# Token operands of the first MLP projection taken from PSUM in product order, and a new issue order of stores and loads between the two projections

## The chip, the core and the metric

The kernel runs on one core of one Trainium2 chip. The metric is device time in microseconds (us) of one execution; the median of the runs is what is compared. The engines are called by their names: TensorE (PE in the profile, its weight loads PEld), VectorE (DVE), ScalarE (ACT), GpSimd (POOL) and SyncE (SP), whose queue issues every DMA of this kernel.

## What is computed

One layer of a hybrid trunk over 1024 tokens of width 1024, in float32. A token mixer (causal pooling groups and a chunked gated delta net) comes first; nothing of it changes here. The part in question is what follows it:

```python
h = h + mix @ w_out
u = rms_norm(h, norm_mlp)                              # 1024 tokens x 1024
h = h + square(relu(u @ w_up)) @ w_down                # 1024 x 4096, then back
return rms_norm(h, norm_final)
```

## The kernel before, in words

**Products.** Each float32 matrix product is made of three passes on TensorE: an operand is split into a rounded part (`wh`, `th`) and the rest (`wl`, `tl`), both in a 32-bit matmul format, and `mm3` multiplies high by high, high by low and low by high. Each of the two MLP projections is done by a scheme with seven block products in place of eight (as Strassen's and Winograd's): the 2 x 2 blocks are the two halves of the tokens (512 each), of the contracted dimension and of the outputs.

**First projection.** The 4096 hidden units come in 16 pairs `p` of 2 x 128. A product is called (p, i), i = 1 to 7: four blocks of 128 rows, three matmuls each, so 12 matmuls of 128 x 128 by 128 x 512. Its weights are made per product by `up_ready`: sums and differences of the four blocks of the raw tile `wu` (in place), then `split` into `wh` (ScalarE cast, L932) and `wl` (VectorE subtraction, L933). Its tokens, `TH[i]` and `TL[i]`, are made once and serve all pairs. `TH[1], TL[1], TH[2], TL[2]` come from the first half of the tokens (`turn_first`). The other five need the second half: `turn_second` turns the normalised tokens `xn` with 32 matmuls on the identity (L48) into eight PSUM banks, ScalarE copies each bank out, weighed by the norm (L914, tiles `r12` and `r22`), VectorE and GpSimd form the differences (L916 and L918 on VectorE, L919 and L920 on GpSimd), and for each i ScalarE casts to `th` (L926) and VectorE subtracts to `tl` (L927).

**Order.** TensorE's queue is in program order. The other engines' queues were put in order by a scheduler when the program was built, and each runs strictly in that order. The list `order` says: (0,1), (1,1), (0,2), (1,2), then the turn, then 6, 7, 5, 4, 3 for pairs 0 and 1 in turn; from pair 2 on 1, 6, 2, 7, 5, 4, 3. A pair has three accumulating banks; the ends of the products give `p1`, `h11`, `u2`, `u3`, `s1`, `s2`, `s4`, which are stored to a DRAM scratch `hd` by `keep` (L960). Small tiles come from the pool `cp` ("c", 9 buffers).

**Second projection.** For i = 1, 2, 5, 6, 7, 3, 4 and eight steps s each, `down_load` brings the raw weights `w` (512 KB, L1069) and the stored hidden values `x` (512 KB, from `hd`, L1072). Both, like the stores, stand in SyncE's one queue. The first step (1, 0) is split in halves (`wh`, `wl`), the others whole (`sh`, `sl`, `th`, `tl`).

Of the kernel before, what the change touches and what calls it, by code (L numbers as in the profile page):

```python
# [28 lines left out]
def hybrid_trunk(ctx, tc, x, norm_mix, w_in, conv_w, w_pool, pool_scale, a_log, dt_bias,  # L29
# [859 lines left out]
    R[12], R[2] = (u3(f"r{n}", F32) for n in (12, 2))  # L889

# [11 lines left out]

    def turn_second(ys):

        R[22] = [c_tile("r22") for _ in range(4)]

        def block(r, j):
            return R[22][j] if r == 22 else R[r][:, j, :]
# [12 lines left out]
        for i, r in ((6, 2), (7, 12), (5, 11), (4, 21), (3, 22)):  # L921
            TH[i] = (big_tile(f"th{i}", [4, HALF], F32R) if i in (5, 4) else
                     u2p.tile(ub, F32R, name="th3", tag="r21") if i == 3 else u3(f"th{i}", F32R))
            TL[i] = big_tile("tl3", [4, HALF], F32R) if i == 3 else u3(f"tl{i}", F32R)
            for j in range(4):
                A.copy(TH[i][:, j, :], block(r, j))  # L926
                V.tensor_tensor(TL[i][:, j, :], block(r, j), TH[i][:, j, :].bitcast(F32), op=ALU.subtract)  # L927
# [14 lines left out]
    def up_ready(p, i):  # L942

        r = raws[p]
        a11, a12, a21, a22 = r[:, :4, :P], r[:, 4:, :P], r[:, :4, P:], r[:, 4:, P:]
        if i == 1:
            G.tensor_tensor(a21, a21, a22, op=ALU.add)
        if i == 6:
            G.tensor_tensor(a11, a21, a11, op=ALU.subtract)
        src = {1: a11, 2: a12, 3: a12, 4: a22, 5: a21, 6: a11, 7: a11}[i]  # L950
        if i == 7:
            G.tensor_tensor(a11, a22, a11, op=ALU.subtract)
        out = split(src, [P, 4, P], ws, "wh", "wl", 5)
        made2.add((p, i))
        if i in (2, 6) and {(p, 2), (p, 6)} <= made2:
            G.tensor_tensor(a12, a12, a11, op=ALU.subtract)
        return out

    def keep(p, i, t):
        nc.sync.dma_start(out=hd[p // 2][i][:, p % 2, :], in_=t)  # L960
# [5 lines left out]
    def combine(p):  # L966

        m = tmp.pop(p)
        h11, h21, h22, h12 = m["h11"], m["p1"], m["u3"], m["u2"]
        s1, s2, s4 = c_tile("s1"), c_tile("s2"), c_tile("s4")  # L970
        V.tensor_tensor(s1, h12, h22, op=ALU.add)
        keep(p, 5, s1)
        V.tensor_tensor(s2, s1, h11, op=ALU.subtract)
        keep(p, 6, s2)
        V.tensor_tensor(h12, h11, h12, op=ALU.subtract)
        keep(p, 7, h12)
        V.tensor_tensor(s4, h21, s2, op=ALU.subtract)
        keep(p, 3, s4)

    def up_product(p, i, w):  # L980
# [14 lines left out]
        elif i == 6:  # L995
            m["u2"] = ws.tile([P, HALF], F32, name="u2", tag="raw", bufs=3)
            V.tensor_tensor(m["u2"], acc, m["p1"], op=ALU.add)
        elif i == 7:
            m["u3"] = c_tile("u3") if p == 1 else ws.tile([P, HALF], F32, name="u3", tag="raw", bufs=3)
            V.tensor_tensor(m["u3"], acc, m["p1"], op=ALU.add)  # L1000
        elif i == 5:
            V.tensor_tensor(m["u3"], acc, m["u3"], op=ALU.add)
            hidden(m["u3"], m["u3"])
            keep(p, 4, m["u3"])
        elif i == 4:
# [3 lines left out]
        else:  # L1009
            V.tensor_tensor(m["u2"], acc, m["u2"], op=ALU.add)  # L1010
            hidden(m["u2"], m["u2"])
# [7 lines left out]
    first = {}  # L1019
    for n, e in enumerate(order):  # L1020
        if e != "turn" and e[0] not in first:
            first[e[0]] = n
# [22 lines left out]
    close(cpc)  # L1045
# [10 lines left out]
    w2c, w2 = opened(name="wr2", bufs=4, reuse_waits="tile")  # L1056
# [96 lines left out]
    close(w2c)  # L1153
# [34 lines left out]
```

## Time and profile before

| | us |
|---|---|
| median of 3 runs | 1172.87 (1172.27 to 1178.7) |
| the profiled execution | 1173.46 |
| its span in the trace | 1171.7 |
| TensorE busy | 1099.8 (94%) |
| VectorE busy | 786.6 (67%) |
| ScalarE busy | 602.8 (51%) |
| GpSimd busy | 327.1 (28%) |

The first projection runs from 514 us to 851 us of the span, the second from there to the end. A row of the timeline has the start, the duration, the engine, the line, the operation and, in brackets, how long the engine had been idle before it and what ended that. Where a row ends in x4 or the like, four instructions in a row are merged, and the duration is from the start of the first to the end of the last. Busy matmul time overlaps itself (a matmul of 0.39 us starts 0.23 us after the one before), so a product is measured from start to start.

### The profile page before, as it was taken

To read this page: it belongs to the slowest core of one execution; us is meant where nothing else is said; L and a number is where in the kernel's file an instruction comes from. 1 tells how busy PE (TensorE), PEld (TensorE's weight loads), DVE (VectorE), ACT (ScalarE), POOL (GpSimd) and SP (SyncE) were. 2 spreads that over 40 slices of the span, in tenths; PEclk is the share of its full clock that TensorE was granted. 3 is DMA by queue.
4 is the path that set the end of the run, shared out by engine and by line. 5 is a ranking of instruction groups with operands and counts; after the bars stand their busy time and mean duration, and the time that the engine had idled before them with its cause. 6 is when DMAs were issued, how large, how long until landed. Compare 5 with 4: busy or idle time off the path is not lost.

```text
span 1171.7 us, 15587 instructions
## 1 busy us (share of the span) xinstructions
PE 1099.8 (94%) x5606; PEld 893.7 (76%) x5606; DVE 786.6 (67%) x1224; ACT 602.8 (51%) x1117; POOL 327.1 (28%) x288
## 2 busy tenths in 40 slices
PE   6998999988898999995999999999979999999997
PEld 5777777767687788773788888888868888888886
DVE  5698698878879775559646454545455597465584
ACT  6666566566565554635545454545443333334353
POOL 7033365465754431045132323131100000000010
PEclk9999999999999999997999999999989999999999
DMA  5233211111213321121344444444298797256561
GB/s 161 81 101 116 61 52 41 55 55 43 66 41 126 109 72 37 37 72 54 133 155 153 147 150 152 145 153 145 81 361 294 262 394 242 90 195 192 189 215 72
DMA packets 93047, 155.23 MB, mean 132 GB/s; under 512 B 7781, under 2 KB 45738, under 8 KB 92970
## 3 DMA queue, kind: packets, MB, share of 16 engines
q1 hardware_dynamic: 92970, 154.24, 39.1%
q8 instruction: 44, 0.72, 0.2%
q14 instruction: 33, 0.27, 0.1%
HBM read 120.66 MB, written 33.55 MB: 132 GB/s over the span
## 4 chain that ended last, share of the span: by engine, by line
PE 71%; DVE 12%; ACT 3%; issue 2%; POOL 2%; DMA 0%; POOLq 0%; DVEq 0%; ACTq 0%; SPq 0%
PE bank L44 53%; PE acc L44 17%; DVE cy L391 2%; DVE tl L927 1%; DVE nxt L410 1%; DVE xx L592 1%; PE bank L48 1%; DVE nxt L409 0%; DMA x<-hd 0%; DVE r L918 0%; ACT th L172 0%; DVE ul L173 0%; DVE ml L764 0%; DVE m L546 0%; DVE kn L533 0%
## 5 line engine op out<-in xcount | busy, mean ns | idle before, releaser
L44 PE MATMUL bank<-th,wh 128*128 128x512 f32 x448 | 178.3, 398 | 11.7 <-ACT th L926 10.7
L44 PE MATMUL bank<-tl,wh 128*128 128x512 f32 x448 | 178.1, 398 | 3.0 <-DVE tl L927 2.9
L44 PE MATMUL bank<-th,wl 128*128 128x512 f32 x448 | 177.5, 396 | 2.2 <-DVE wl L933 2.2
L932 ACT CAST sh<-x 128x1024 fp32r<-128x1024 f32 x55 | 57.9, 1054 | 160.9 <-PE bank L44 154.2
L44 PE MATMUL bank<-th,sh 128*128 128x512 f32 x344 | 133.8, 389 | 0.0
L44 PE MATMUL bank<-th,sl 128*128 128x512 f32 x344 | 133.8, 389 | 0.0
L44 PE MATMUL bank<-tl,sh 128*128 128x512 f32 x344 | 133.8, 389 | 0.0
L44 PE MATMUL acc<-uh,wh 128*128 128x512 f32 x320 | 130.4, 407 | 1.1 <-DVE ul L173 0.6
L44 PE MATMUL acc<-ul,wh 128*128 128x512 f32 x320 | 129.3, 404 | 0.0
L932 ACT CAST wh<-wu 128x512 fp32r<-128x512 f32 x112 | 69.1, 621 | 116.0 <-PE bank L44 98.2
L44 PE MATMUL acc<-uh,wl 128*128 128x512 f32 x320 | 128.8, 402 | 0.0
L933 DVE TENSOR_TENSOR sl<-x,sh 128x1024 fp32r<-128x1024 f32 x55 | 67.3, 1223 | 88.1 <-ACT sh L932 88.0
L933 DVE TENSOR_TENSOR wl<-wu,wh 128x512 fp32r<-128x512 f32 x112 | 80.4, 722 | 45.0 <-ACT wh L932 45.0
L44 PEld LDWEIGHTS bank<-th,wh 128*128 128x128 f32 x448 | 85.1, 190 | 32.0 <-ACT th L926 11.4
L44 PEld LDWEIGHTS bank<-tl,wh 128*128 128x128 f32 x448 | 85.0, 190 | 24.5 <-DVE tl L927 5.4
L44 PEld LDWEIGHTS bank<-th,wl 128*128 128x128 f32 x448 | 85.1, 190 | 22.3 <-DVE wl L933 3.1
L152 POOL TENSOR_TENSOR stf<-stf,mhalf 128x1 f32<-128x1 f32 x8 | 7.9, 998 | 329.7 <-DVE stf L1125 329.7
L588 POOL TENSOR_TENSOR bl<-m,lev 128x512 f16<-128x512 f16 x48 | 62.0, 1291 | 82.5 <-PE bank L44 70.2
L391 DVE SCALAR_TENSOR_TENSOR cy<-cr,cols,cy 128x512 f32<-128x512 f32 x72 | 74.1, 1034 | 8.2 <-ACT cy L389 7.7
L133 POOL TENSOR_TENSOR wl<-raw,wh 128x512 fp32r<-128x512 f32 x48 | 68.0, 1421 | 36.4 <-ACT wh L132 36.2
L44 PEld LDWEIGHTS bank<-th,sl 128*128 128x128 f32 x344 | 64.6, 188 | 13.5
L44 PEld LDWEIGHTS bank<-th,sh 128*128 128x128 f32 x344 | 64.6, 188 | 13.5
(325 smaller groups left out, 2372.1 us busy)
## 6 DMA issues: line engine op xcount, KB each, us to landing
w<-in_w_down_dram SPq DMA_DIRECT2D x72, 512.0 KB, 6.9
x<-hd SPq DMA_DIRECT2D x56, 512.0 KB, 3.3
raw<-in_w_in_dram SPq DMA_DIRECT2D x80, 256.0 KB, 2.7
wu<-in_w_up_dram SPq DMA_DIRECT2D x16, 1024.0 KB, 5.4
hd<-s SPq DMA_DIRECT2D x48, 256.0 KB, 2.0
hd<-u SPq DMA_DIRECT2D x32, 256.0 KB, 2.1
raw<-in_w_out_dram SPq DMA_DIRECT2D x24, 256.0 KB, 2.8
xin<-in_x_dram SPq DMA_DIRECT2D x8, 512.0 KB, 5.1
```

The source lines that it names most:

```text
L44: T0.matmul(out, lhsT, rhs, start=start, stop=stop, skip_group_check=goes_on)
L48: T0.transpose(out, in_, identity)
L133: eng.tensor_tensor(lo, raw, hi.bitcast(F32), op=ALU.subtract)
L152: last["rsqrt"] = G.tensor_tensor(s, s, mhalf[:, :n], op=ALU.pow)
L391: V.scalar_tensor_tensor(cy, cr[:, e:e + HALF], tap[e], cy, op0=ALU.mult, op1=ALU.add)
L410: V.tensor_tensor(nxt[:, n:], cur[:, n:], cur[:, :W - n], op=ALU.add)
L588: G.tensor_tensor(bl, m1, bc(lev[l]), op=ALU.mult)
L592: V.tensor_tensor(xx, px, bc(ident), op=ALU.add)
L927: V.tensor_tensor(TL[i][:, j, :], block(r, j), TH[i][:, j, :].bitcast(F32), op=ALU.subtract)
L932: A.copy(hi, src)
L933: V.tensor_tensor(lo, src, hi.bitcast(F32), op=ALU.subtract)
```

## The change

In `up_ready` the sums and differences of the weight blocks are moved from GpSimd to VectorE for pairs 0 and 1, and the weight parts of (0,1) and (1,1) come from the "c" pool. `turn_second` stands ahead of (0,2) and (1,2) now. The differences are taken by VectorE straight from PSUM, in one instruction that weighs the bank and subtracts (`weighed`, L908), and operand 3 is split from PSUM (`weigh`, L172 and L173). The operands are made in the order 6 with 3, then 5, 7, 4, by functions that stand between the products; GpSimd has none of it. The order of the products is 6, 5, 3, 7, 4 for pairs 0 and 1 and 1, 6, 2, 5, 7, 3, 4 from pair 2 on, with `v5` in the place of `u3`. Of the last pair only the first store is issued at once, the others are kept for after the first loads of the second projection, and the pool `w2` of that projection is opened at its first use.

```diff
+TH[3], TL[3], TH[6], TL[6] = (u3(nm, F32R) for nm in ("th3", "tl3", "th6", "tl6"))
+def weighed(r, k, x):
+    V.scalar_tensor_tensor(r, turned_banks[k], nmlp[:, k:k + 1], x, op0=ALU.mult, op1=ALU.subtract)
+def parts_of(i, src):
+    for j in range(4):
+        A.copy(TH[i][:, j, :], src[j])
+        V.tensor_tensor(TL[i][:, j, :], src[j], TH[i][:, j, :].bitcast(F32), op=ALU.subtract)
 def turn_second(ys):
     for k in range(KT):
-        pt = acc_bank() if k < 2 else work_bank()
+        pt = turned_banks[k] = acc_bank() if k in (0, 1, 6, 7) else work_bank()
         turn(ys, k, pt)
         j = k % 4
-        A.activation(block(12 if k < 4 else 22, j), pt, AF.Copy, scale=nmlp[:, k:k + 1])
         if k < 4:
-            V.tensor_tensor(R[11][:, j, :], R[12][:, j, :], R[11][:, j, :], op=ALU.subtract)
+            A.activation(R[12][:, j, :], pt, AF.Copy, scale=nmlp[:, k:k + 1])
+            weighed(R[11][:, j, :], k, R[11][:, j, :])
         else:
-            V.tensor_tensor(R[2][:, j, :], R[22][j], R[11][:, j, :], op=ALU.subtract)
-            G.tensor_tensor(R[12][:, j, :], R[22][j], R[12][:, j, :], op=ALU.subtract)
-            G.tensor_tensor(R[21][:, j, :], R[21][:, j, :], R[2][:, j, :], op=ALU.subtract)
-    for i, r in ((6, 2), (7, 12), (5, 11), (4, 21), (3, 22)):
...
+            weighed(R[2][:, j, :], k, R[11][:, j, :])
+    parts_of(6, rows_of(2))
+    for j in range(4):
+        weigh(turned_banks[4 + j], 4 + j, TH[3][:, j, :], TL[3][:, j, :], nmlp)
+def operands_5():
+    TH[5], TL[5] = (big_tile(f"t{m}5", [4, HALF], F32R) for m in "hl")
+    parts_of(5, rows_of(11))
+def operands_7():
+    for j in range(4):
+        weighed(R[12][:, j, :], 4 + j, R[12][:, j, :])
+    R[4] = [c_tile("r4") for _ in range(4)]
+    for j in range(4):
+        V.tensor_tensor(R[4][j], R[21][:, j, :], R[2][:, j, :], op=ALU.subtract)
+    TH[7], TL[7] = u3("th7", F32R), big_tile("tl7", [4, HALF], F32R)
+    parts_of(7, rows_of(12))
+def operands_4():
+    TH[4], TL[4] = u2p.tile(ub, F32R, name="th4", tag="r21"), u3("tl4", F32R)
+    parts_of(4, R[4])
 def up_ready(p, i):
+    eng = V if p < 2 else G
     if i == 1:
-        G.tensor_tensor(a21, a21, a22, op=ALU.add)
+        eng.tensor_tensor(a21, a21, a22, op=ALU.add)
...
+    if i == 1 and p < 2:
+        out = split(src, [P, 4, P], cp, "c", "c", 9)
+    else:
+        out = split(src, [P, 4, P], ws, "wh", "wl", 5)
...
 def keep(p, i, t):
+    if p == NPAIR - 1 and i != 1:
+        late.append((p, i, t))
+    else:
+        store(p, i, t)
...
-order = [(0, 1), (1, 1), (0, 2), (1, 2), "turn"]
-order += [(0, 6), (1, 6), (0, 7), (1, 7), (0, 5), (1, 5), (0, 4), (1, 4), (0, 3), (1, 3)]
+order = [(0, 1), (1, 1), lambda: turn_second(ys), (0, 2), (1, 2), operands_5, (0, 6), (1, 6), operands_7,
+         (0, 5), (1, 5), (0, 3), (1, 3), operands_4, (0, 7), (1, 7), (0, 4), (1, 4)]
 for p in range(2, NPAIR):
-    order += [(p, i) for i in (1, 6, 2, 7, 5, 4, 3)]
+    order += [(p, i) for i in (1, 6, 2, 5, 7, 3, 4)]
...
-w2c, w2 = opened(name="wr2", bufs=4, reuse_waits="tile")
+            if n and "w2" not in pools:
+                close(cpc)
+                pools["w2c"], pools["w2"] = opened(name="wr2", bufs=4, reuse_waits="tile")
...
+        while late:
+            store(*late.pop(0))
```

VectorE's queue around the operand of product 6, before: `tl6` is the low part of that operand, `r11`, `r2` and `r22` are differences and weighed blocks, `tl7` and `tl5` the low parts for products 7 and 5.

```order
L916 TENSOR_TENSOR r11_5485<-r12_5783,r11_5485 128x512 x4
L918 TENSOR_TENSOR r2_5784<-r22_5944,r11_5485 128x512
L918 TENSOR_TENSOR r2_5784<-r22_5945,r11_5485 128x512
L918 TENSOR_TENSOR r2_5784<-r22_5946,r11_5485 128x512
L918 TENSOR_TENSOR r2_5784<-r22_5947,r11_5485 128x512
L927 TENSOR_TENSOR tl6_6013<-r2_5784,th6_6012 128x512 x4
L927 TENSOR_TENSOR tl7_6023<-r12_5783,th7_6022 128x512 x4
L927 TENSOR_TENSOR tl5_6033<-r11_5485,th5_6032 128x512 x4
```

The same place after: the second quarter of `tl6`, nine instructions for products 3, 7, 5 and 4 (`tl3`, `r12`, a weight part `wl`, `r4`), and the third quarter; two more stand before the fourth.

```order
L913 TENSOR_TENSOR tl6_5788<-r2_5784,th6_5787 128x512
L173 SCALAR_TENSOR_TENSOR tl3_5786<-bank_5930,cols_209,th3_5785 128x512
L908 SCALAR_TENSOR_TENSOR r12_5783<-bank_5930,cols_209,r12_5783 128x512
L173 SCALAR_TENSOR_TENSOR tl3_5786<-bank_5936,cols_209,th3_5785 128x512
L908 SCALAR_TENSOR_TENSOR r12_5783<-bank_5936,cols_209,r12_5783 128x512
L955 TENSOR_TENSOR wl_6044<-wu_5852,wh_6043 128x512
L943 TENSOR_TENSOR r4_6066<-r21_5484,r2_5784 128x512
L943 TENSOR_TENSOR r4_6067<-r21_5484,r2_5784 128x512
L943 TENSOR_TENSOR r4_6068<-r21_5484,r2_5784 128x512
L943 TENSOR_TENSOR r4_6069<-r21_5484,r2_5784 128x512
L913 TENSOR_TENSOR tl6_5788<-r2_5784,th6_5787 128x512
```

So the four quarters of `tl6`, which stood together, are spread, and GpSimd's subtractions (L919, L920) have become VectorE's L908 and L943.

SyncE's queue at the end of the first projection, before: `hd7_i` are stores of the last two pairs, `w` and `x` loads of the second projection.

```order
L960 DMA hd7_1_5839<-h11_8327 128x512
L960 DMA hd7_4_5842<-u3_8347 128x512
L960 DMA hd7_2_5840<-p1_8289 128x512
L1069 DMA w_8431<-in_w_down_dram 128x2x512
L1072 DMA x_8433<-hd0_1_5790 128x1024
L1069 DMA w_8435<-in_w_down_dram 128x2x512
L1072 DMA x_8437<-hd1_1_5797 128x1024
```

The same place after.

```order
L994 DMA hd7_1_5843<-h11_8323 128x512
L994 DMA hd7_4_5846<-v5_8344 128x512
L1103 DMA w_8417<-in_w_down_dram 128x2x512
L1106 DMA x_8419<-hd0_1_5794 128x1024
L1103 DMA w_8421<-in_w_down_dram 128x2x512
L1106 DMA x_8423<-hd1_1_5801 128x1024
```

The store of `p1`, which stood ahead of the first load, stands behind the first eight loads now, with four others; the one store of the last pair's later products that is still ahead is that of `v5`.

## Rows read from the trace of the kernel before

**Rows 1.** The page: busy time, share of the span, instructions.

```profile
PE 1099.8 (94%) x5606; PEld 893.7 (76%) x5606; DVE 786.6 (67%) x1224; ACT 602.8 (51%) x1117; POOL 327.1 (28%) x288
```

**Rows 2.** Waits, 440 to 600 us, then 820 to 1171: total us, times, longest.

```profile
PE bank L44 <- ACT th L926: 10.7, 2, 6.4
PE bank L44 <- DVE tl L927: 2.9, 2, 2.4
PE bank L44 <- ACT p L990: 1.0, 1, 1.0
...
PE bank L44 <- ACT wh L932: 6.2, 1, 6.2
```

**Rows 3.** Timeline of TensorE, start of the first projection.

```profile
515.13 0.51 PE L44 MATMUL bank<-th,wl 128*128 128x512 f32 x1 [0.93 <-DVE wl L933]
...
519.50 0.50 PE L44 MATMUL bank<-th,wl 128*128 128x512 f32 x1 [1.32 <-DVE wl L933]
...
527.40 1.04 PE L48 MATMUL acc<-ident,xn 128*128 128x128 f32 x8
...
537.43 0.79 PE L44 MATMUL bank<-th,wh 128*128 128x512 f32 x1 [6.38 <-ACT th L926]
...
553.48 0.77 PE L44 MATMUL bank<-th,wh 128*128 128x512 f32 x1 [4.35 <-ACT th L926]
...
561.14 0.40 PE L44 MATMUL bank<-th,wh 128*128 128x512 f32 x1
...
577.86 0.40 PE L44 MATMUL bank<-th,wh 128*128 128x512 f32 x1
...
584.49 0.50 PE L44 MATMUL bank<-th,wh 128*128 128x512 f32 x1 [0.96 <-ACT p L990]
```

**Rows 4.** Timeline of VectorE, the same stretch and the earlier turn.

```profile
482.99 1.40 DVE L173 SCALAR_TENSOR_TENSOR tl<-bank,cols,th 128x512 fp32r<-128x512 f32 x2
...
515.69 0.15 DVE L156 TENSOR_SCALAR st<-st 128x1 f32<-128x1 f32 x1 [0.62 <-ACT xn L155]
...
538.79 13.94 DVE L927 TENSOR_TENSOR tl<-r,th 128x512 fp32r<-128x512 f32 x12
...
555.05 1.89 DVE L927 TENSOR_TENSOR tl<-r,th 128x512 fp32r<-128x512 f32 x3
```

**Rows 5.** Timeline of GpSimd, the same stretch.

```profile
543.32 3.42 POOL L920 TENSOR_TENSOR r<-r,r 128x512 f32<-128x512 f32 x2
...
588.74 1.30 POOL L949 TENSOR_TENSOR wu<-wu 128x512 f32<-128x512 f32 x1 [11.79 <-DVE wl L933]
```

**Rows 6.** Stretches: length, busy us by engine, granted clock, DMA share, GB/s.

```profile
550.00:555.00 5.00, 1.52 (x4) 1.26 (x5) 4.97 (x9) 2.18 (x5) 0.00 (x0) 0.62 0.00 0
555.00:560.00 5.00, 5.00 (x17) 3.96 (x16) 3.83 (x7) 2.15 (x6) 0.00 (x0) 0.70 0.01 3
854.00:856.00 2.00, 0.00 (x0) 0.00 (x0) 1.44 (x3) 0.24 (x1) 0.00 (x0) 0.73 1.01 399
```

**Rows 7.** Timelines of TensorE, SyncE, ScalarE and VectorE between the two projections.

```profile
850.34 0.39 PE L44 MATMUL bank<-th,wl 128*128 128x512 f32 x1
856.95 0.79 PE L44 MATMUL bank<-wh 128*128 128x512 f32 x1 [6.22 <-ACT wh L932]
...
850.43 0.39 SPq L1069 DMA_DIRECT2D w<-in_w_down_dram  x1
850.87 0.49 SPq L1072 DMA_DIRECT2D x<-hd  x1
...
852.15 0.63 ACT L964 ACTIVATE u<-u 128x512 f32<-128x512 f32 x1
855.76 0.62 ACT L932 CAST wh<-x 128x512 fp32r<-128x512 f32 x1 [2.98 <-DMA x<-hd]
860.06 1.22 DVE L933 TENSOR_TENSOR sl<-x,sh 128x1024 fp32r<-128x1024 f32 x1
```

**Rows 8.** Timeline of VectorE, one pair of the steady part.

```profile
823.10 0.69 DVE L1000 TENSOR_TENSOR u<-bank,p 128x512 f32<-128x512 f32 x1 [1.64 <-PE bank L44]
```

More of the change, by code (lines that the diff above doesn't have):

```diff
@@ L901, in c_tile, with rows_of @@
         return cp.tile([P, HALF], F32, name=nm, tag="c")
+    turned_banks = {}
+    def weighed(r, k, x):
[4 more added lines that the diff above has]
+            V.tensor_tensor(TL[i][:, j, :], src[j], TH[i][:, j, :].bitcast(F32), op=ALU.subtract)
+    def rows_of(r):
+        return [R[r][:, j, :] for j in range(4)]
     def turn_second(ys):
-        R[22] = [c_tile("r22") for _ in range(4)]
@@ L921, in turn_second @@
-        for i, r in ((6, 2), (7, 12), (5, 11), (4, 21), (3, 22)):
[L922 to L927, printed above, removed]
+                A.activation(R[12][:, j, :], pt, AF.Copy, scale=nmlp[:, k:k + 1])
@@ L945, in up_ready, with store @@
         a11, a12, a21, a22 = r[:, :4, :P], r[:, 4:, :P], r[:, :4, P:], r[:, 4:, P:]
+        eng = V if p < 2 else G
         if i == 1:
-            G.tensor_tensor(a21, a21, a22, op=ALU.add)
+            eng.tensor_tensor(a21, a21, a22, op=ALU.add)
         if i == 6:
-            G.tensor_tensor(a11, a21, a11, op=ALU.subtract)
+            eng.tensor_tensor(a11, a21, a11, op=ALU.subtract)
         src = {1: a11, 2: a12, 3: a12, 4: a22, 5: a21, 6: a11, 7: a11}[i]
         if i == 7:
-            G.tensor_tensor(a11, a22, a11, op=ALU.subtract)
-        out = split(src, [P, 4, P], ws, "wh", "wl", 5)
+            eng.tensor_tensor(a11, a22, a11, op=ALU.subtract)
+        if i == 1 and p < 2:
+            out = split(src, [P, 4, P], cp, "c", "c", 9)
+        else:
+            out = split(src, [P, 4, P], ws, "wh", "wl", 5)
         made2.add((p, i))
         if i in (2, 6) and {(p, 2), (p, 6)} <= made2:
-            G.tensor_tensor(a12, a12, a11, op=ALU.subtract)
+            eng.tensor_tensor(a12, a12, a11, op=ALU.subtract)
         return out
+    late = []
     def keep(p, i, t):
+        if p == NPAIR - 1 and i != 1:
+            late.append((p, i, t))
+        else:
+            store(p, i, t)
+    def store(p, i, t):
         nc.sync.dma_start(out=hd[p // 2][i][:, p % 2, :], in_=t)
@@ L997, in up_product @@
             V.tensor_tensor(m["u2"], acc, m["p1"], op=ALU.add)
+        elif i == 5:
+            m["v5"] = c_tile("v5") if p == 1 else ws.tile([P, HALF], F32, name="v5", tag="raw", bufs=3)
+            V.tensor_tensor(m["v5"], acc, m["p1"], op=ALU.add)
         elif i == 7:
[L999 to L1005, printed above, removed]
+            V.tensor_tensor(m["v5"], acc, m["v5"], op=ALU.add)
+            hidden(m["v5"], m["v5"])
+            keep(p, 4, m["v5"])
+        elif i == 3:
+            V.tensor_tensor(m["u2"], acc, m["u2"], op=ALU.add)
+            hidden(m["u2"], m["u2"])
+        else:
             V.tensor_tensor(m["p1"], acc, m["p1"], op=ALU.add)
@@ L1008, in up_product @@
             keep(p, 2, m["p1"])
-        else:
-            V.tensor_tensor(m["u2"], acc, m["u2"], op=ALU.add)
-            hidden(m["u2"], m["u2"])
             combine(p)
-    order = [(0, 1), (1, 1), (0, 2), (1, 2), "turn"]
-    order += [(0, 6), (1, 6), (0, 7), (1, 7), (0, 5), (1, 5), (0, 4), (1, 4), (0, 3), (1, 3)]
+    order = [(0, 1), (1, 1), lambda: turn_second(ys), (0, 2), (1, 2), operands_5, (0, 6), (1, 6), operands_7,
+             (0, 5), (1, 5), (0, 3), (1, 3), operands_4, (0, 7), (1, 7), (0, 4), (1, 4)]
     for p in range(2, NPAIR):
-        order += [(p, i) for i in (1, 6, 2, 7, 5, 4, 3)]
+        order += [(p, i) for i in (1, 6, 2, 5, 7, 3, 4)]
     LEAD = 2
[L1019 to L1022, printed above, removed]
     ready = {}
-    todo = [e for e in order if e != "turn"]
+    todo = [e for e in order if not callable(e)]
     loaded = done_n = 0
@@ L1030, in get_ready @@
             p, i = todo[done_n]
-            while loaded <= min(p + 1, NPAIR - 1):
+            while loaded <= min(max(p + (p > 1), 1), NPAIR - 1):
                 up_load(loaded)
@@ L1034, in get_ready @@
             ready[(p, i)] = up_ready(p, i)
+            if (p, i) == (0, 4):
+                up_load(loaded)
+                loaded += 1
             done_n += 1
@@ L1038, in hybrid_trunk @@
     for e in order:
-        if e == "turn":
-            turn_second(ys)
+        if callable(e):
+            e()
             continue
@@ L1066, in down_load @@
         for n, blk in enumerate(LOADS[i]):
-            t = (wr if n == 0 else w2).tile(pair2, F32, name="w", tag="w")
+            if n and "w2" not in pools:
+                close(cpc)
+                pools["w2c"], pools["w2"] = opened(name="wr2", bufs=4, reuse_waits="tile")
+            t = (pools["w2"] if n else wr).tile(pair2, F32, name="w", tag="w")
             e, c = blk // 10 - 1, blk % 10 - 1
```

7 lines of the change are left out of this document (2 added, 5 removed).

## The prediction, made before the changed kernel ran

> **What bounds the kernel now.** I read the page's busy shares first, then the waits, then the timelines of the two places where TensorE waits, stretch by stretch. TensorE is busy for 94% of the span [rows 1], so time can come only from its few gaps, or be lost by opening new ones. The waits show the gaps that the change touches [rows 2]: 10.7 us in two waits for the token cast (L926), 2.9 for the low token parts (L927), 1.0 for the copy `p1`, and one of 6.2 us between the projections. In TensorE's timeline [rows 3] the reader is to see where they lie: after the turn (527.40 and the 3.6 us behind it) it stands for 6.38 us until product (0,6) starts at 537.43, again for 4.35 until (0,7) at 553.48. The cause is on VectorE: twelve low parts take 13.94 us [rows 4], while three in a row later take 1.89, because GpSimd's subtractions at 1.7 us each run beside the former [rows 5]. [...] Behind that stretch TensorE runs product on product: from 561.14 to 577.86, the start of (2,1), six products take 2.79 us each [rows 3].
>
> **The turn, worked out.** Durations on VectorE with GpSimd silent: a two-operand subtraction starts (1.89 - 0.68) / 2 = 0.60 us after the one before; one that reads PSUM, 1.40 - 0.75 = 0.66 [rows 4]. In the new kernel GpSimd has nothing between its last `st` and the load of pair 2, so these hold throughout.
>
> The start is unchanged: the square behind the last token's `st` ends at 515.7 [rows 4]. Two things stand ahead on VectorE now: the weight part of (0,2) before that of (0,1), which moves TensorE's first stall from 515.13 to 515.74 (0.6 lost), and from 515.78 on a chain without a gap. Up to the low part of (1,1): two sums, the `xn` of the last token (0.67) and one more sum, 2.47 us, so it is ready at 518.95 against 519.50 in TensorE's row before [rows 3]. (1,1) ends at 521.4 and the turn starts there, not at 527.40. Its seventh and eighth block wait for the two `acc` banks, which VectorE must have read: VectorE comes to the first of these at 523.66, so TensorE loses 0.65 and ends the turn at 525.54. (0,2) and (1,2) follow, which now stand beside the making of the operands: 5.5 us, to 531.03.
>
> (0,6) needs the four quarters of `tl6`. By VectorE's new order, from 515.78 to the third quarter stand 23 subtractions (13.8), the `xn` (0.67) and 12 reads of PSUM (7.92): it starts at 538.17 and is ready at 538.86; the fourth after one subtraction and two reads of PSUM, at 540.78. The first two are there at 531.42 and 532.62. So TensorE does seven matmuls of (0,6), stands from 533.5 to 538.9 (5.4 us), and 0.5 us more for the last quarter. A gap of that length halves the clock as the 4.35 did [rows 6], and I take eight matmuls at half of it, 0.2 us more each. (0,6) ends at 541.8 and (1,6) at 545.4. Here the old 6.38 has become 5.4, but behind it the 4.35 is gone: `tl5` was made in the chain, `tl3` is ready at 541.4, and (0,3) needs VectorE's read of (0,5), after 15 more instructions, at 550.5, which TensorE reaches at 545.4 + 2 x 2.79 = 551.0. That margin of 0.5 us is the narrowest behind the gap. `th7` and `tl7` are 10 us early. From 545.4 eight products to (2,1): 22.3, so 567.7 where it was 577.86 [rows 3]: **10.2 us gained**.
>
> The load of pair 2 is issued after the weight part of (0,4), by 552.6; it has 15 us until 567.7. The stall of 0.96 at 584.49 [rows 3] comes from a `p1` tile that waits for a store of pair 0; that store (`s2`) is now issued at 564, seven us before the copy that needs its place: **1.1 us gained** with the restart.
>
> The moved operations' price: seven of the eight block sums stand in the chain. The trace shows none on VectorE. Its nearest row is the subtraction at 0.60, which I take; from above GpSimd's own 1.30 for the same tiles [rows 5], 4.9 us more in all, and 1.72 under company, 7.8 more; from below nothing, since the operation has the same two operands and size. L908 I take as L173 (0.66).
>
> [...]
>
> **Between the projections.** Let E be the end of TensorE's last product, 850.7 [rows 7]. Before, the first `w` and `x` are issued at 850.43 and 850.87, behind the store of `p1`, whose squares end at about E; `x` is cast at 855.76 and TensorE starts at 856.95 = E + 6.2. After, they stand behind the store of `v5`, which is complete after the fifth of seven products, 5.5 us before E; with its sum and two passes of ScalarE (2.0) the loads go out at E - 3.0 and E - 2.6. The 4.9 us from issue to cast in the old rows (850.87 to 855.76), with three more loads beside it, is the upper bound for the landing: E + 2.3. ScalarE, though, has the two passes of the last `p1` ahead, which end at E + 2.05. I take the cast at E + 1.95 and, by the old distance of 1.2 us from cast to TensorE, the start at E + 3.1: **3.1 us gained** (2.8 by the upper bound, 5.2 if the shorter gap leaves the clock up, which cost 2.1 behind the old one, ten matmuls at half of it; 1.0 if the loads are slowed by the stores). The last part of the second step was ready at 861.3 [rows 7], E + 10.6; with its loads 2.7 us and more earlier it is ready by E + 7.9 and is needed 24 matmuls behind the start, at E + 8.6.
>
> [...]
>
> **Sum.** 10.2 + 1.1 + 3.1 = 14.4. From the profiled execution's 1173.46 (span 1171.7 and 1.8 around it) that is 1159.1; that run stands 0.6 above the median of 1172.87, so 1158.5 for the median.
>
> **Rivals.**
> A. VectorE's chain is slower than 0.60 a step, by the bounds of the moved sums (4.9 to 7.8). The gap in (0,6) grows by as much, the (0,3) margin is gone. For it: none of these sums was ever seen on VectorE. Against: the same shape in the weight parts. Gain 6.6 to 9.5: 1165.
> B. The clock stays up between the projections (2.1) and some of the waits in (0,6) are shorter: 1155. For it: 3 us is the shortest of these gaps. Against: the gaps of 4.35 and 6.22 us both brought it down [rows 6].
> C. The change does not do what it says. The order rows show the second half of `tl6` behind parts of 3, 7, 5 and 4, so product 6 is not served first. Should ScalarE, which runs two steps ahead in my count, fall behind VectorE, the gap takes back both old waits (10.7 in place of 5.4, and 3 of clock and (0,3)): a gain of about 6 is left at most, 1168 to 1171.
> D. Slower. In the steady part VectorE now takes `s1` before the sum of `p1`, and `s1` waits for ScalarE's passes on `u2`; the weight parts of the next pair queue behind. Every one of 14 pairs would stall TensorE; from 1.03 us a pair (14.4 / 14) the gain is gone, and at 1.5 a pair the time is 1179.5. Against it: before, VectorE stands 1.64 us waiting for TensorE at the same kind of place [rows 8].
>
> **How the numbers follow.** Forecast 0.58, A 0.17, B 0.10, C 0.09, D 0.06. A change under 0.5% (5.9 us) can't be told from none. The forecast, A and B are faster by more (0.85), C is within (0.09), D slower (0.06). The range goes from B with 3 us of further gain in the turn (1152) to the far end of A (1167); the forecast's own is 1155 to 1162.
>
> **What would show it.** Right: one long wait of TensorE for a low part `tl` inside (0,6), of 4 to 7 us, none before (0,3) or (0,7); GpSimd without work from 517 to 552; (2,1) at 566 to 570; no wait for `p1` at (2,2); a gap of 3 to 4 us between the projections, ended by ScalarE's cast. Wrong: L970 to L982 on VectorE at over 0.8 us, a second wait behind (0,6), gaps in TensorE between 590 and 820, or a gap between the projections that ends with a load.

## The result and the profile after

The changed kernel takes 1162.74 us in the median (1160.21 to 1164.51), beside 1172.59 for the kernel before: a ratio of 0.9902, 95% interval 0.9878 to 0.9927. It is faster, by 9.9 us where 14.4 were forecast. The profiled execution took 1163.48 us, its span is 1161.8. The page's busy shares, to compare with [rows 1]: GpSimd gave up 24 us of work, and TensorE's busy time grew by 1.1 us though it has the same 5606 instructions.

```profile
PE 1100.9 (95%) x5606; PEld 893.6 (77%) x5606; DVE 789.8 (68%) x1240; ACT 601.5 (52%) x1113; POOL 303.5 (26%) x272
```

TensorE's waits in the same stretches as [rows 2] (total us, times, longest):

```profile
PE bank L44 <- DVE tl L913: 5.8, 3, 5.3
PE bank L44 <- DVE c L955: 1.7, 2, 1.5
...
PE bank L44 <- ACT p L1024: 0.3, 1, 0.3
PE acc L48 <- DVE r L908: 0.3, 1, 0.3
...
PE bank L44 <- ACT wh L954: 3.2, 1, 3.2
```

The two waits for `th` (10.7 us) are gone, one wait for a low part of 5.3 us is left, and the gap between the projections is 3.2 in place of 6.2. TensorE's timeline, for [rows 3] and the first rows of [rows 7]; beside the waits it has the first matmul of (0,1), (2,1), (3,1), (15,1) and the last one of the projection:

```profile
515.01 0.39 PE L44 MATMUL bank<-th,c 128*128 128x512 f32 x1
517.16 0.73 PE L44 MATMUL bank<-th,c 128*128 128x512 f32 x2 [1.53 <-DVE c L955]
522.81 1.04 PE L48 MATMUL acc<-ident,xn 128*128 128x128 f32 x8
525.88 1.31 PE L48 MATMUL acc<-ident,xn 128*128 128x128 f32 x8 [0.29 <-DVE r L908]
540.34 0.80 PE L44 MATMUL bank<-tl,wh 128*128 128x512 f32 x1 [5.27 <-DVE tl L913]
542.26 0.79 PE L44 MATMUL bank<-tl,wh 128*128 128x512 f32 x1 [0.27 <-DVE tl L913]
568.99 0.39 PE L44 MATMUL bank<-th,wh 128*128 128x512 f32 x1
574.99 0.50 PE L44 MATMUL bank<-th,wh 128*128 128x512 f32 x1 [0.33 <-ACT p L1024]
588.97 0.40 PE L44 MATMUL bank<-th,wh 128*128 128x512 f32 x1
823.61 0.40 PE L44 MATMUL bank<-th,wh 128*128 128x512 f32 x1
842.93 0.39 PE L44 MATMUL bank<-th,wl 128*128 128x512 f32 x1
846.54 0.79 PE L44 MATMUL bank<-wh 128*128 128x512 f32 x1 [3.22 <-ACT wh L954]
```

VectorE's timeline, for [rows 4]: two of the moved weight sums (L975 and L982), the read of four turned banks, the four `r4`, which GpSimd made before, and the third and fourth quarter of `tl6` behind them.

```profile
522.07 0.69 DVE L975 TENSOR_TENSOR wu<-wu 128x512 f32<-128x512 f32 x1
522.67 0.69 DVE L982 TENSOR_TENSOR wu<-wu 128x512 f32<-128x512 f32 x1
...
526.40 2.72 DVE L908 SCALAR_TENSOR_TENSOR r<-bank,cols,r 128x512 f32<-128x512 f32 x4
...
537.19 2.49 DVE L943 TENSOR_TENSOR r<-r,r 128x512 f32<-128x512 f32 x4
539.60 0.68 DVE L913 TENSOR_TENSOR tl<-r,th 128x512 fp32r<-128x512 f32 x1
...
541.52 0.68 DVE L913 TENSOR_TENSOR tl<-r,th 128x512 fp32r<-128x512 f32 x1
```

GpSimd, for [rows 5], and the clock by stretches, for [rows 6]:

```profile
559.52 1.30 POOL L970 TENSOR_TENSOR wu<-wu 128x512 f32<-128x512 f32 x1 [41.24 <-DMA wu<-in_w_up_dram]
```

```profile
535.00:540.00 5.00, 0.07 (x1) 0.00 (x0) 5.00 (x9) 1.92 (x5) 0.00 (x0) 0.84 0.28 105
540.00:545.00 5.00, 4.39 (x10) 3.00 (x11) 5.00 (x9) 4.59 (x9) 0.00 (x0) 0.50 0.00 0
545.00:550.00 5.00, 5.00 (x23) 4.15 (x22) 5.00 (x9) 0.99 (x2) 0.00 (x0) 0.98 0.00 0
847.00:852.00 5.00, 4.97 (x12) 3.60 (x12) 4.72 (x6) 4.11 (x6) 0.00 (x0) 0.50 1.03 379
```

From TensorE's starts in the two profiles the whole difference of the spans can be put down to stretches. The column of before needs three starts that are not among its rows: 513.58 for (0,1), 598.43 for (3,1), 831.23 for (15,1).

| stretch of TensorE | before | after | difference | forecast |
|---|---|---|---|---|
| up to (0,1) | 513.58 | 515.01 | +1.43 | 0 |
| (0,1) to (2,1): turn and operands | 64.28 | 53.98 | -10.30 | -10.2 |
| (2,1) to (3,1): first steady pair | 20.57 | 19.98 | -0.59 | -1.1 |
| (3,1) to the last matmul: 13 pairs | 251.91 | 253.96 | +2.05 | 0 |
| last matmul to the second projection | 6.61 | 3.61 | -3.00 | -3.1 |
| from there to the end | 314.75 | 315.26 | +0.51 | 0 |
| sum | 1171.7 | 1161.8 | -9.90 | -14.4 |

So the terms of the forecast came out to about half a microsecond or better, though in the first steady pair that is half of the term, and two stretches that had no term took back 3.5 us. The first of these, ahead of everything that changes, lies for the most part in the clock: in 275 to 290 us it was granted 1.00 in the profile of before and 0.77 in that of after. The first row is of before, the second of after:

```profile
275.00:290.00 15.00, 12.70 (x99) 11.44 (x97) 11.06 (x28) 8.07 (x18) 4.02 (x4) 1.00 0.12 35
```

```profile
275.00:290.00 15.00, 12.73 (x82) 11.78 (x81) 8.00 (x21) 5.82 (x10) 2.87 (x3) 0.77 0.13 34
```

It isn't the change's: in the profiles of the twelve kernels below (0,1) starts anywhere from 510.9 to 515.7 us, in either direction; e2, whose code up to there is that of the changed kernel, starts it at 510.91. The runs of the changed kernel alone spread over 4.3 us, so the experiments are read by stretches, counted from (0,1), and by times second.

### The profile page after: what moved, and what is told of

Its sections match the earlier page's. It is cut to its first block, busy times and chain, and to the rows that moved or that the text cites. A ratio compares the mean times of both kernels' runs of the same rounds, so it can differ in the third digit from the quotient of the medians.

```text
span 1161.8 us, 15593 instructions
## 1 busy us (share of the span) xinstructions
PE 1100.9 (95%) x5606; PEld 893.6 (77%) x5606; DVE 789.8 (68%) x1240; ACT 601.5 (52%) x1113; POOL 303.5 (26%) x272
## 4 chain that ended last, share of the span: by engine, by line
PE 70%; DVE 13%; ACT 3%; issue 2%; POOL 1%; DMA 1%; POOLq 0%; DVEq 0%; ACTq 0%
PE bank L44 52%; PE acc L44 18%; DVE cy L391 2%; DVE nxt L410 1%; DVE xx L592 1%; PE bank L48 1%; DVE wl L955 1%; DVE nxt L409 0%; DMA wu<-in_w_up_dram 0%; DVE r L908 0%; DVE tl L913 0%; ACT th L172 0%; DVE ul L173 0%; DMA raw<-in_w_out_dram 0%; DVE kn L533 0%
## 5 line engine op out<-in xcount | busy, mean ns | idle before, releaser
L44 PE MATMUL bank<-tl,wh 128*128 128x512 f32 x440 | 175.3, 398 | 5.8 <-DVE tl L913 5.8
L44 PE MATMUL bank<-th,wh 128*128 128x512 f32 x440 | 175.2, 398 | 0.3 <-ACT p L1024 0.3
L44 PE MATMUL bank<-th,wl 128*128 128x512 f32 x440 | 174.7, 397 | 0.0
L955 DVE TENSOR_TENSOR wl<-wu,wh 128x512 fp32r<-128x512 f32 x110 | 84.4, 768 | 28.4 <-ACT wh L954 26.8
```

The source lines that it names most:

```text
L44: T0.matmul(out, lhsT, rhs, start=start, stop=stop, skip_group_check=goes_on)
L955: V.tensor_tensor(lo, src, hi.bitcast(F32), op=ALU.subtract)
```

## The experiments

Times of before on the chips of these runs: 1173.3 to 1174.0 in the median. "Turn" is the time from (0,1) to (2,1) on TensorE, 53.98 us after; "gap" the longest wait between the projections, 3.22 after.

**e1: old order of products from pair 2 on.**

```diff
...
-        order += [(p, i) for i in (1, 6, 2, 5, 7, 3, 4)]
+        order += [(p, i) for i in (1, 6, 2, 7, 5, 4, 3)]   # sums after 3, "v5" begun by 7
```

> The changed kernel with one part undone: from pair 2 on the products run in the old order 1, 6, 2, 7, 5, 4, 3 again (7 writes the tile that 5 completes, the sums follow 3). Measured so far: of the forecast 14.4 us the profile after gives back 2.1 us in the steady part, where a product takes 2.80 us from start to start in most places, against 2.75 to 2.78 before (14 pairs of 7: 0.02 us each on the mean). Theory 1, the order of the products sets that pace: here the products 1, 6, 2, 7 are at 2.75 again in three pairs of four, the steady part from (2,1) to the end of the last product takes 271.9 us as before in place of 274.0, and the time falls by 2 us to about 1160.7. Rival, the pace hangs on where the token operands lie or on the state in which the turn leaves TensorE: then it stays at 2.80 and the time at 1162.7. Both leave the gap of 5.3 us in (0,6) and the gap of 3.2 us between the projections as they are.

1162.23 us (ratio 0.9905, 0.9878 to 0.9931). (2,1) to the last matmul: 270.48 in place of 273.94, products of 2.75 in the places 1, 6, 2. Theory 1 holds so far, and the 3.5 us were given back at the end: the gap is 4.20, 1.0 longer, and what follows it takes 2.4 us more, with the clock at half for longer (0.50 in 841 to 846, 0.67 in 846 to 851) and a second wait of 1.22 us. Here no load waits for a tile, all go out at once, and the first x, issued at 834.07, is cast 5.6 us later (SyncE's and ScalarE's timelines):

```profile
834.07 0.49 SPq L1121 DMA_DIRECT2D x<-hd  x1
...
839.66 0.62 ACT L954 CAST wh<-x 128x512 fp32r<-128x512 f32 x1 [0.96 <-DMA x<-hd]
```

**e2: stores of the last pair at once.**

```diff
-        if p == NPAIR - 1 and i != 1:
-            late.append((p, i, t))
-        else:
-            store(p, i, t)
+        store(p, i, t)
```

> The changed kernel with one part undone: the stores of the last pair are issued as they come, none is kept for after the first loads. In SyncE's queue the first x then stands behind the store of s1, and the next x behind the stores of s2, p1, u2 and s4. Theory: s1 is ready 0.05 us after the end E of the last product, so the first x is issued at about E + 0.5 in place of E - 2.6, is cast some 4 to 5 us later in place of E + 2.0, and the gap between the projections grows from 3.2 us to 5 to 6.5, with the rest of the parts 2 to 3 us late too: 2 to 4 us slower, 1165 to 1167. Rival, ScalarE's squares and not the loads set that gap: it stays at 3.2 to 4 us and the time within 1 us of 1162.7. The other rival, that the transfers are slowed by the stores among them anyway: also within 1 us.

1165.34 us (ratio 0.9936, 0.9911 to 0.9961), 2.6 slower than after in the median, with intervals that overlap. The gap is 5.95, with x issued at 839.84 behind the store of s1 and cast at 844.22. The theory holds for the gap, where the kept stores are worth 2.7 us. In the profiles 1.1 us of that come back behind it, where the clock is at half for less long (1.00 from 850 on, where after has 0.50 in 847 to 852), so from (0,1) to the end 1.8 us are left.

**e3: the weight sums of pairs 0 and 1 on GpSimd.**

```diff
-        eng = V if p < 2 else G
+        eng = G
```

> The changed kernel with one part undone: the eight sums and differences of weight blocks for pairs 0 and 1 are on GpSimd again. VectorE's chain loses seven instructions of 0.60 us (4.2 us), but GpSimd's instructions of 1.3 to 1.7 us run beside it from 513 to about 530. Theory 1, two-operand instructions of VectorE are slowed by GpSimd beside them (1.16 to 1.43 us in the kernel before against 0.60): the eight to ten of them in that stretch lose 0.5 to 0.8 us each, 4 to 8 us in all, GpSimd's own chain feeds the weight parts late, and nothing is gained: time 1161 to 1168, with VectorE's mean in that stretch over 0.9 us. Rival, the work on VectorE is what counts and the slowing is small: the gap of 5.3 us in (0,6) shrinks to 1 to 2 us and the time falls to about 1158.

1163.80 us (ratio 0.9921, 0.9894 to 0.9949); the turn takes 57.16, 3.2 more. VectorE has fewer instructions and is later. In its timeline beside GpSimd's sums an `xn`, which took 0.75 in the profile after, takes 1.79, and a weight part up to 1.78; from 525.4, where GpSimd has stopped, instructions of that shape take 0.67 again:

```profile
516.14 1.79 DVE L163 TENSOR_SCALAR xn<-h,st 128x1024 f32<-128x1024 f32 x1
517.85 1.78 DVE L955 TENSOR_TENSOR wl<-wu,wh 128x512 fp32r<-128x512 f32 x1
...
523.14 1.09 DVE L955 TENSOR_TENSOR wl<-wu,wh 128x512 fp32r<-128x512 f32 x1
...
526.13 0.67 DVE L913 TENSOR_TENSOR tl<-r,th 128x512 fp32r<-128x512 f32 x1
```

Reads of PSUM (L908) keep their 0.74 us there. Theory 1 holds. Rival A of the forecast falls by the profile after: with GpSimd silent the moved sums start 0.60 us apart (522.07 and 522.67 above).

**e9: the turn behind (0,2) and (1,2) again.**

```diff
-order = [(0, 1), (1, 1), lambda: turn_second(ys), (0, 2), (1, 2), operands_5, ...
+order = [(0, 1), (1, 1), (0, 2), (1, 2), lambda: turn_second(ys), operands_5, ...
```

> The changed kernel with one part undone: the turn stands behind (0,2) and (1,2) again. Theory, those two products cover the making of the operands: without them TensorE has nothing to do from the turn's end, about 532 by the clock of the profile after, until the first quarter of tl6; VectorE comes to its first read of a turned bank 4 to 5 us later (530 in place of 525) and its 26 instructions from there to the last quarter of tl6 take 16.4 us: ready at 546.5 in place of 542.2. (0,6) ends some 4.5 us later, and the clock is at half for longer: 1167 to 1169. Rival, VectorE's chain is full of weight parts up to 525 anyway and makes up for the later turn: within 2 us of 1162.7.

1168.82 us (ratio 0.9956, 0.9941 to 0.9971); the turn takes 59.72, 5.7 more, with four waits in (0,6) of 1.7, 3.4, 3.4 and 0.9 us. Undone by itself, this one move costs more than half of the 10.3 us gained in the turn; e3's part, undone by itself, costs 3.2.

**e4: operand of product 6 first.** No instruction is added; an edge of order puts the parts of operand 3 and the sums for 7 behind the last quarter of `tl6`.

```diff
+        with tc.issue_after(made["V", 6].ins), tc.issue_after(made["A", 6].ins):
+            for j in range(4):
+                weigh(turned_banks[4 + j], 4 + j, TH[3][:, j, :], TL[3][:, j, :], nmlp)
...
+        with tc.issue_after(made["V", 6].ins):      # r12 for product 7; r4 behind the last of these
```

> The changed kernel with VectorE's and ScalarE's order altered at one place: the parts of operand 3 and the sums for operand 7 are queued behind the last quarter of the operand of product 6, and the four r4 behind those. Nothing is added or taken away. Theory: the third and fourth quarter of tl6 come out at about 533 and 534 in place of 540.3 and 542.2, when TensorE needs them at 534.9 and 535.6, so the gap of 5.3 us, the 0.3 behind it and the 2 us at half clock vanish; VectorE's work is then late at the next place, its read of (0,5) ahead of (0,3), with a wait of 1 to 2 us. (0,3) starts at 543.5 to 545 in place of 552.4: 7 to 8 us gained, 1154.5 to 1156. Rival, VectorE's chain as a whole is the limit, whatever its order: what is saved in (0,6) comes back at (0,3), (0,7) or at the load of pair 2, and less than 3 us are gained: 1160 or more.

1160.20 us (ratio 0.9886, 0.9862 to 0.9910); the turn takes 50.82. The 5.3 us wait is gone, but only 3.2 us are gained. In front of (0,3) TensorE waits for `v5`, and behind that the clock falls (TensorE's timeline, then stretches):

```profile
546.63 0.50 PE L44 MATMUL bank<-th,wh 128*128 128x512 f32 x1 [2.23 <-DVE v L1037]
```

```profile
545.00:550.00 5.00, 3.37 (x10) 2.70 (x11) 5.00 (x9) 2.79 (x6) 0.00 (x0) 0.79 0.01 3
550.00:555.00 5.00, 5.00 (x21) 4.01 (x20) 4.99 (x9) 1.77 (x3) 0.00 (x0) 0.87 0.60 191
```

(0,3) started 5.2 us earlier than after, counted from (0,1), where the theory had 7.4 or more, and 2.1 of these were lost again behind it. The theory was right on the place of the next wait; it was too high by some 2 us in what (0,6) gives and by the half clock that it had left out.

**e5: the read of (0,5) ahead of `r4`.**

```diff
+    def operands_7b():
+        with tc.issue_after(made["v5", 0].ins):     # r4, th7, tl7
...
+             (0, 5), operands_7b, (1, 5), (0, 3), (1, 3), operands_4, (0, 7), (1, 7), (0, 4), (1, 4)]
```

> The kernel of e4 with VectorE's order altered once more: the four r4 stand behind the first v5 (the read of (0,5) that (0,3) waits for) instead of in front of it. Nothing is added. In e4 TensorE stood 2.23 us before (0,3) for that read, which came behind r4 (2.4 us) and five others, and the clock was at half for 3.4 us behind it. Theory, the wait is only a matter of order: v5 comes out at E4's 546.5 less 2.4, so (0,3) starts 2 us earlier with no wait over 0.5 us, the clock stays up, and (2,1) starts 46.9 us after the first product of the first projection in place of 50.8: 3.9 us gained, 1156.3. Rival, VectorE is simply full until 550: the parts tl7 are late at (0,7) by what was saved, and (2,1) stays within 1 us of 50.8.

1155.41 us (ratio 0.9851, 0.9837 to 0.9866); the turn takes 47.33. The wait for `v5`, at 545, is 0.67 us, and the clock stays at 1.00 from 530 to 555. So the theory of order holds, and "VectorE is full" falls: the changed kernel's own rest of 5.3 us was order, not work.

**e6: e5 with the old order for pairs 2 to 14.**

```diff
...
+        order += [(p, i) for i in ((1, 6, 2, 7, 5, 4, 3) if p < NPAIR - 1 else (1, 6, 2, 5, 7, 3, 4))]
```

> The kernel of e5, and from pair 2 to pair 14 the products in the old order 1, 6, 2, 7, 5, 4, 3 (e1 showed 270.5 us from (2,1) to the end of the last product in place of 273.9); the last pair keeps the new order, since in e1 the old order at the end let all loads of the second projection go out at once, the first x took 5.6 us to land and the gap grew from 3.2 to 4.2 us. Theory, the pace goes with the order and the gap with the last pair: products of 2.75 in the places 1, 6, 2, a gap of 3.2 to 3.5 us, and 3 us less than e5: 1153. Rival, the pace hangs on the state in which the turn leaves TensorE (the pattern of its starts locks in at another place once the turn has no stall): then it is at 2.80 or between, and the time within 1 us of e5.

1152.60 us (ratio 0.9823, 0.9807 to 0.9840): 271.17 us from (2,1) to the last matmul where e5 has 274.31, a gap of 3.2. The theory holds. The rival, that the turn sets the pace, falls by all profiles together: with the new order and the operands where the changed kernel has them a pair takes 19.55 us in after, e2, e3, e4, e5 and e9, though their turns take 47.3 to 59.7 us, and with the old order 19.30 us in e1, e6, e7, e11 and e12.

**e8: the kernel before with the new order of products from pair 2 on.**

```diff
...
-        order += [(p, i) for i in (1, 6, 2, 7, 5, 4, 3)]
+        order += [(p, i) for i in (1, 6, 2, 5, 7, 3, 4)]   # "u3" begun by 5, sums after 4
```

> The kernel before with one part of the change alone: from pair 2 on the products run in the new order 1, 6, 2, 5, 7, 3, 4 (5 writes the tile that 7 completes, the sums follow 4). Theory, the order sets the pace of TensorE: all products but the fourth go to 2.80 us, and from (2,1) to the end of the last product 274 us pass, as in the changed kernel, in place of 272.7 with a wait of 1.0 in the first of these pairs: 1.5 to 2 us lost there, 1174 to 1175. It also takes s1 and s2 earlier, so the wait of 1.0 us at (2,2) goes or shrinks. Rival, the pace belongs to where the changed kernel keeps its token operands: then the products stay at 2.75 to 2.78 with one pair in four at 2.80, and the time at 1172 to 1173. The gap between the projections shrinks in either case only by what the earlier stores give, and the gaps at the turn stay 6.4 and 4.35 us.

1169.33 us (ratio 0.9968, 0.9957 to 0.9980): the other way from what I had expected, and my theory of e1, that the order by itself sets the pace, falls. The pace is not 19.55 us a pair but 19.37, even a little under the 19.40 of before. The gain is in the gap, 3.61 us with the stores issued at once: in this kernel the new order of the last pair alone brings 2.6 of the 3.0 us that the gap lost. The wait of 1.0 at (2,2) stays. TensorE's timeline, first matmul of (3,1) and of (15,1):

```profile
597.26 0.39 PE L44 MATMUL bank<-th,wh 128*128 128x512 f32 x1
...
829.66 0.39 PE L44 MATMUL bank<-th,wh 128*128 128x512 f32 x1
```

**e10: e5 with the operands of products 3 and 5 in each other's places.**

```diff
-    TH[3], TL[3], TH[6], TL[6] = (u3(nm, F32R) for nm in ("th3", "tl3", "th6", "tl6"))
+    TH[5], TL[5], TH[6], TL[6] = (u3(nm, F32R) for nm in ("th5", "tl5", "th6", "tl6"))
...
-        TH[5], TL[5] = (big_tile(f"t{m}5", [4, HALF], F32R) for m in "hl")
+            TH[3], TL[3] = (big_tile(f"t{m}3", [4, HALF], F32R) for m in "hl")
```

> The kernel of e5 (new order of products in every pair) with the token operands of product 3 and product 5 in each other's places in SBUF; instructions and order of the steady part are the same. e8 showed that the order alone doesn't make the pace: the same order took 19.37 us a pair in the kernel before, 19.55 in the changed one, with the operands at other addresses. Theory, the pace goes with the addresses: a pair moves away from 19.55 us by 0.1 or more, up to 3 us over the 14 pairs. Rival, it goes with the order and with what the other engines do beside it, not with these addresses: 19.55 us stay, within 0.03, and the time stays within 1 us of 1155.4.

1152.31 us (ratio 0.9817, 0.9797 to 0.9837), 3.1 under e5 in the median; from (2,1) to the last matmul it is 270.68 in place of 274.31. The same rows, in this kernel:

```profile
583.24 0.39 PE L44 MATMUL bank<-th,wh 128*128 128x512 f32 x1
...
814.84 0.39 PE L44 MATMUL bank<-th,wh 128*128 128x512 f32 x1
```

(814.84 - 583.24) / 12 = 19.30 us a pair, where after has (823.61 - 588.97) / 12 = 19.55. In the traces of e5 and e10 every engine runs the same instructions in the same order from (3,1) on; two operands have exchanged their places, and the pace goes from 19.55 to 19.30. So it goes with the place of the operands and with the order together.

**e7: casts ahead of the passes on `p1`.**

```diff
...
+        if n == 0:
+            ready[todo[0]] = down_ready(*todo[0])
...
+            with tc.issue_after(made["hi"].ins):
+                end_pair(NPAIR - 1)                   # the two passes on p1 and the sums
```

> The kernel of e6, with the last two passes of ScalarE for the last pair (p1) and the sums behind them queued behind the four casts of the first step of the second projection. Theory of the forecast: the gap between the projections is set by ScalarE, which has p1's two passes (1.3 us, and 0.8 of waiting for p1) ahead of the first cast, while the first x is there earlier. Then the first cast comes when x lands, 3.5 to 4.7 us after its issue, in place of E + 2.0, and the gap of 3.2 us shrinks to 1.5 to 2.7: 0.5 to 1.7 us less than e6, 1151 to 1152. Rival, x lands at E + 2 anyway: the gap stays at 3.2 us, ended by the cast that waits for the load, and the time at 1152.6.

1154.28 us (ratio 0.9834, 0.9816 to 0.9852), from (0,1) on within 0.4 us of e6, the gap 3.21. The first cast now waits for x, and starts 4.69 us after the issue of that load (SyncE's and ScalarE's timelines):

```profile
830.89 0.50 SPq L1131 DMA_DIRECT2D x<-hd  x1
...
835.58 0.62 ACT L959 CAST wh<-x 128x512 fp32r<-128x512 f32 x1 [2.76 <-DMA x<-hd]
```

The rival holds. ScalarE and the load end together, and my forecast had named one of them.

**e11: e7 with ten small tiles in place of nine.**

```diff
-    cpc, cp = opened(name="cp", bufs=9, reuse_waits="tile")
+    cpc, cp = opened(name="cp", bufs=10, reuse_waits="tile")
...
```

> The kernel of e7 with ten buffers of the small tiles (c) in place of nine. Forecast: the stall at (2,2) came from p1 waiting for a tile whose store was late, and the change was to remove it (1.1 us); the profile after still shows 0.3 us there, e5 and e6 0.7 to 0.8, since everything ahead became earlier but the stores of pair 0 didn't. Theory: with one more buffer p1 waits for an earlier store, the wait of 0.7 us in the first pair of the steady part goes and the time falls by 0.7 us against e7, to 1150.5 to 1151.5. Rival, p1's copy comes late for another reason (ScalarE's queue): the wait stays at 0.7 us and the time at that of e7.

1152.70 us (ratio 0.9822, 0.9807 to 0.9837). The wait at (2,2) goes from 0.8 to 0.6 us only; the rest of the difference to e7 lies ahead of (0,1) (512.7 in place of 514.6) and at the clock behind the gap. The tile is not what that copy mainly waits for, and the rival holds: in e7 and in e11 the copy stands without idle time behind three casts in ScalarE's queue, the first of which has waited 1.25 us for a weight sum of GpSimd. ScalarE's timeline in e11, and the same place in the kernel before, where the cast ahead of the copy has waited 2.13 us for TensorE:

```profile
564.37 1.66 ACT L959 CAST wh<-wu 128x512 fp32r<-128x512 f32 x3 [1.25 <-POOL wu L980]
565.94 0.58 ACT L1029 COPY p<-bank 128x512 f32<-128x512 f32 x1
```

```profile
583.34 0.62 ACT L932 CAST wh<-wu 128x512 fp32r<-128x512 f32 x1 [2.13 <-PE bank L44]
583.86 0.58 ACT L990 COPY p<-bank 128x512 f32<-128x512 f32 x1
```

**e12: loads and casts ahead of the last pair's end.** e6 with the old order in the last pair too.

```diff
...
+            with tc.issue_after(made["hi"].ins), tc.issue_after(made["lo"].ins):
+                end_pair(NPAIR - 1)                   # last sum u2, its passes, s1 to s4
+            with tc.issue_after(made["x0"].ins):      # stores behind the first x
+                while late:
+                    store(*late.pop(0))
```

> The kernel of e6 with the old order of products in the last pair too, and with its end changed: the stores of its v5 and p1 stand behind the first loads of the second projection, and the last sum u2, its two passes on ScalarE and the sums behind it are queued behind the casts and subtractions of the first step. e7 showed that taking ScalarE's passes away alone changes nothing, since x landed 4.7 us after its issue and that came to the same E + 2.0. Theory: both bounds have to go together. Here the first w and x go out behind the store of h11, at about E - 8.8 and E - 8.3, are there by E - 3.5, and the casts follow p1's passes from E - 0.75: TensorE starts at about E + 0.5 and waits 1 us more for the low parts, 1.3 to 1.8 us in all in place of 3.2, and if no single wait is over 1.5 us the clock stays up (2 us). Time 1148.5 to 1150.5. Rival, the parts of the second step are late now (its w still waits for the tile that the last but one product reads, and lands at E + 2): a wait of 2 to 3 us moves to the 25th matmul, and the time stays within 1 us of 1152.6.

1148.80 us (ratio 0.9790, 0.9767 to 0.9812): faster than both kernels. The first x goes out 8.9 us before the last product ends, the cast follows `p1`'s passes without a wait, TensorE waits 0.39, 0.31 and 0.24 us, and the clock stays up (timelines of SyncE, ScalarE and TensorE, then stretches):

```profile
822.97 0.48 SPq L1132 DMA_DIRECT2D x<-hd  x1
...
831.07 0.60 ACT L959 CAST wh<-x 128x512 fp32r<-128x512 f32 x1
...
832.25 0.50 PE L44 MATMUL bank<-wh 128*128 128x512 f32 x1 [0.39 <-ACT wh L959]
```

```profile
832.00:837.00 5.00, 4.20 (x16) 2.96 (x17) 5.00 (x8) 5.00 (x8) 0.00 (x0) 1.00 1.04 408
```

## Why the prediction was right, and where it was not

*The number.* The median of 1162.74 lies 0.7 us above the 1155 to 1162 that the forecast gave for itself, and inside the whole range of 1152 to 1167. That range reached so high only for rival A, whose slow sums did not come; that the result lies in it is in part luck. What was right is the mechanism of the turn and the start of the second projection. Of the 4.5 us that are missing, 2.05 lie in the steady pairs, 1.43 ahead of the change, and about half a microsecond each at (2,2) and behind the gap.

*The turn: right, step by step.* Counted from the first matmul of (0,1), 513.58 in the forecast's clock and 515.01 in the profile after: the turn was to start 7.8 us later and did (522.81); the third quarter of `tl6` was to be ready at 25.28 and the fourth at 27.20, and they were at 25.27 and 27.19 (539.60 and 541.52, 0.68 each); the wait was to be 5.4 and is 5.27; (2,1) was to come at 54.1 and came at 53.98. The first stall grew by the 0.6 that was named (0.93 to 1.53). Only the stall in the turn is 0.29 where 0.65 were taken, and the rest of the turn took that much longer, so that the turn's 4.14 us came out by two errors that cancel. What carried this was counting VectorE's queue in its new order, at durations taken where GpSimd was silent; e3 shows what those durations would have been otherwise. No wait stood before (0,3) or (0,7), and GpSimd was idle to 559.

*Operands still spread: the rest that the forecast saw and took as given.* The 5.3 us and the half clock behind them (0.84 and 0.50, with matmuls that don't wait 0.43 us apart in place of 0.23) are the price of nine instructions between two quarters of `tl6`; e4 and e5 take it out by order alone, 6.7 us in the turn.

*(2,2): right in sign, by a wrong cause, and too large.* 0.6 of 1.1 us came, and a wait of 0.33 remains. The forecast had the copy `p1` wait for an old store. In the profile of before no such wait is to be seen: the copy starts directly behind a cast that has waited for TensorE (583.34 and 583.86, under e11), and one more tile, in e11, took only 0.2 us off the wait. What holds the copy is its place in ScalarE's queue.

*Between the projections: the time right, the cause half right.* The start was to be at E + 3.1 and came 3.22 us after the last product. The forecast had ScalarE's passes as what ends the gap and the load as an upper bound. e7 shows that the load ends it at the same moment: taking the passes away brings nothing. Both had to go, which e12 does. The old row's 4.9 us from issue to cast, the forecast's upper bound, had six other loads of that size beside it in the trace of before, not three. That e8 has a gap of 3.61 with stores issued at once, and e2 one of 5.95 in the changed kernel, shows that the kept stores matter by which store the scheduler puts ahead of x, as the forecast had read it from SyncE's queue.

*The step that failed: the pace of the steady pairs, put at no change without a reason.* The forecast lets TensorE run "product on product" and its sum has no term for the 13 pairs from (3,1) on; they took 2.05 us more, 19.55 us a pair in place of 19.40. The forecast looked for new waits there (rival D), and there is none: VectorE still waits for TensorE, 1.75 us at the place of [rows 8], and TensorE has no gap. What changed is the interval between matmuls that don't wait. The order of the products is part of it (e1, e6: 19.30 with the old order), but not alone (e8: 19.37 with the new order in the kernel before), and the place of two operands undoes all of it (e10: 19.30 with the new order). The change had altered both: besides the order, `tl5`, `tl7` and `th3`, for example, lie in other pools than before. How the place of an operand acts on the pace, no run here shows.

*Not a step at all:* 1.43 us ahead of the change, for the most part from the clock in another stage; other kernels start (0,1) up to 4.1 us earlier. The remaining 0.51 us lie behind the gap, where TensorE was at half clock for 5.9 us from its start (846.54 to about 852.4), and before for 4.8 us (856.95 to about 861.8).

Of the rivals, A fell with the sums at 0.60 us, B was not seen (the clock fell both times, to 0.50 in 540 to 545 and in 847 to 852), C's mechanism was there in the order but ScalarE did not fall behind (its price was also mis-added: a gain of 6 is 1167, not 1168 to 1171), and D's price of 1.03 us a pair or more was 0.15 by another cause.

## What to carry to other kernels

Count the queue of the engine that makes the operands in its new order, at durations from a stretch with the same neighbours: that gave every start in the turn to 0.4 us. When a wait remains, see first whether work that nobody waits for stands in front of it, since an edge of order adds no instruction; e4 shows that it can move the wait to the next place. And compare the interval of back-to-back matmuls before and after any change of order or of tiles: 0.02 us a product is no wait in any view, and was a fifth of this gain.

## What the runs showed of the hardware that was not expected

- A product of 12 back-to-back matmuls took 2.75 to 2.80 us, in patterns that repeat exactly from pair to pair: 19.30, 19.37, 19.55 us a pair, or in the kernel before three pairs at about 19.35 and each fourth at 19.58. Which of them appears went with the order of the products and with the place of the operands.
- In e3 VectorE's subtractions of two SBUF operands took up to 2.6 times as long beside GpSimd's sums (1.78 us in place of 0.68), and an `xn` 2.4 times (1.79 in place of 0.75); its reads of PSUM with the same output size did not (0.74).
- A wait of 2.23 us after back-to-back matmuls was followed by half clock (0.79 and 0.87 in the stretches of e4); a wait of 1.53 (after, 1.00 in 517 to 522), one of 0.67 (e5, 1.00 to 555) and those of 0.39, 0.31 and 0.24 (e12) were not.
